# Half of a projection stage moves from plain products to seven-product pairs, and another matrix's block sums are spread over two stages

## The chip, the cores and the metric

The kernel runs on one core of one Trainium2 chip. The metric is the device time of one launch in microseconds (us); a run's time is that of one execution, and the times shown are medians of several. "The profile" is a page made from one execution recorded by the hardware profiler, and "the trace" is the record behind it. TensorE appears in it as PE (matmuls) and PEld (weight loads), VectorE as DVE, ScalarE as ACT, GpSimd as POOL, SyncE as SP (it only issues transfers here). L438 means line 438 of the kernel.

## The reference

One inference step of a two-layer hybrid decoder in float32, for 1024 prompt positions and 8 single decode positions, model width 2048. Layer A is a causal pooling mixer, layer B is sliding-window attention over keys and values projected once from layer A's output. Cut to what matters here:

```python
def pool_layer(x, ...):                       # layer A
    z = x @ w_in                              # 2048 -> 4096
    u, gate = z[..., :D_POOL], z[..., D_POOL:]
    d, new_state = multiscale_pool(u, prefix, pos)
    d = einsum(d by groups, w_grp) * scale
    y = (d * silu(gate)) @ w_out              # 2048 -> 2048
    return layer_norm(ALPHA * x + y, g_ln, b_ln), new_state

kv = h @ w_kv                                 # 2048 -> 512; rope on part of each key head

def attn_layer(x, ...):                       # layer B
    z = x @ w_in                              # 2048 -> 4096
    q = rope_partial(z[..., :D_ATTN], pos)
    gate = z[..., D_ATTN:]
    o = attn_core(q, kb, vb, q_pos, k_pos, sinks)   # window 128, 32 heads of 64, a sink per head
    y = (o * silu(gate)) @ w_out              # 2048 -> 2048
    return layer_norm(ALPHA * x + y, g_ln, b_ln)
```

## The kernel before

**Layout and precision.** Activations stand transposed, features on the 128 partitions and positions along the row, in two chunks: chunk 0 has 512 positions, chunk 1 has 520 (512 and the 8 decode positions). A feature block is 128 features; there are 16. Each float32 operand is split into a high part (a ScalarE cast, L423 for weights, L686 for inputs) and a low part (a VectorE subtraction, L438 and L695), and a product is three matmuls: high by high, high by low, low by high.

**Stages.** The list `PHASES` has nine entries: "ai" (layer A's input projection with the pooling), "ao" (its output projection), "bi" (keys, values, queries, gates and attention), "bo" (layer B's output projection), each for chunk 0 and chunk 1; "ai" of chunk 0 is in two parts. What is called the fifth stage is "bi" of chunk 0, the sixth is "bi" of chunk 1, the seventh and eighth are "bo".

**Two ways to multiply.** A unit (`unit`, L614 to L616) computes one output block of 128 features the plain way: two weight tiles of 128 x 1024, 48 matmuls with 512 columns. Two units, a pair of output blocks, can instead be had in 2 x 2 block form (halves of the features in and out, halves of the positions) by seven block products in place of eight (`seven`, L586 to L588; `pair` and `both` call it): seven weight blocks of 128 x 1024, each a quadrant of the weights or a sum of quadrants, seven input blocks, each a quadrant of the inputs or one of four sums T1 to T4, and 168 matmuls of 256 (chunk 1: 260) columns. Results are combined between the products by ScalarE and VectorE. In the kernel before, the first part of "ai" of chunk 0 and the whole fifth stage are plain (`PLAIN`); all else goes by seven products.

**Where the sums come from.** The four weight sums of a pair of blocks are formed once and kept in device memory: for w_in_a in the second part of stage one while they are used (`first_pair`; its additions are L307), for w_kv and w_in_b beside the plain units of the fifth stage (`plain_pair`, L254), for w_out_a and w_out_b by a side task (`sum_gen`, 32 pieces each, L397 to L400). When a later stage loads such a sum, `sums` runs the side task until the sum has been issued. The input sums T1 to T4 are formed by `t_ops` (four VectorE operations, L741 to L744, and a store), either on the fly or by the side task `t_gen`, which loads a stored activation.

**The order of the work.** The program is written out in one order, and `in_order` holds each engine to it. Time is counted in ticks: one tick per product of `seven`, two per weight tile of `unit` (`end`). Weights come through a stream of entries in the order of their use (`build_stream`); `begin`, called once per weight tile or product, issues loads some entries ahead, the casts and low parts fewer ahead: (7, 4, 3) in seven-product stages, (5, 4, 3) in plain ones. Inputs of the next stage are set up by `x_begin`, which first finishes the side task that makes them (`ready`); `x_tick` then loads, casts and splits them tick by tick as buffers are free, and `x_get` makes what is still missing. Side tasks (`self.side`) go one after the other, one step at every `every` ticks when at least `room` buffers are free. All of it lives in 53 buffers of 128 x 1040 floats (`Mem`).

**Attention.** Each query block t has a chain with fixed tick distances (`attend`): scores on TensorE (L1456), selection of the window and maximum (L1473, L1477, L1481), exponentials and norm on ScalarE (L1492, L1505), transposes (L1509), copies (L1518, L1519), products with the values (L1533), and the gate (L1542). Before it `q_done` fetches the rotated halves of the queries by four small transfers (`partner`, L1313, on SP's queue) and applies rope three ticks later (L1321, L1428).

**Queues.** SP issues all loads and the stores of the norms; GpSimd's queue issues the stores of weight sums, input sums and gated outputs. Each queue is in order: a load that waits for its buffer holds back what stands behind it.

Of the kernel before, what the change touches and what calls it, by code (L numbers as in the profile page):

```python
# [50 lines left out]
    ("ai", 0, (0, 1)), ("ai", 0, (1, 4)), ("ai", 1, (0, 4)), ("ao", 0, None), ("ao", 1, None), ("bi", 0, None),  # L51
    ("bi", 1, None), ("bo", 0, None), ("bo", 1, None),
# [40 lines left out]
class Slot:  # L93
# [15 lines left out]
    def free(self, stored=False):  # L109
        self.mem.release(self, 10 if stored else 0)  # L110

# [48 lines left out]
class Kern:  # L160
    def __init__(self, ctx, tc, io):
# [21 lines left out]
        self.posts, self.events, self.side = [], {}, []  # L183
        self.fresh = False
# [108 lines left out]
    def first_pair(self, name, q):  # L293
# [18 lines left out]
        def free(*ks):  # L312
# [5 lines left out]
            2: ent("e", [load("b", a21), load("c", a22)], [add("e", "b", "c", 1)], []),  # L318
# [4 lines left out]
            6: ent("c", [], [], free("c")),  # L323
# [10 lines left out]
    def build_stream(self):  # L334
        io = self.io
        w = []
        for kind, c, part in PHASES:
# [10 lines left out]
            elif kind == "bi":  # L348
                w += self.next_pairs("wkv", range(2), locked) if seven else pr("wkv", 0) + pr("wkv", 1)
                for p in range(8):  # L350
                    if seven:
                        w += pr("wib", p) + pr("wib", 8 + p)
                    else:
# [14 lines left out]
    def sum_gen(self, name):  # L368
# [15 lines left out]
        for n, (q, cs) in enumerate(parts):  # L384
            one = self.ph == "bi1"
            while one and n not in held and len(self.mem.whole()) < 6 and self.hurry is not name:
                yield
            load(n)
            if not one:
                load(n + 1)  # L390
            yield
            if one:
                yield
            s = held.pop(n)
            t = s.v(4, W)
            add = self.nc.vector.tensor_add
            add(t[:, 0:2, :], t[:, 0:2, :], t[:, 1:3, :])  # L397
            add(t[:, 2, :], t[:, 2, :], t[:, 0, :])
# [3 lines left out]
            if n % 4 == 3:  # L402
                self.summed[name] = q + 1
            yield

    def sums(self, name, q):

        self.hurry = name
        while self.summed.get(name, 16) <= q:
            self.side_step()  # L410
        self.hurry = None
# [48 lines left out]
    def end(self):  # L460
# [9 lines left out]
        room = len(self.mem.whole()) - 2 * len(self.xq)  # L470
        if self.side and int(self.i / self.every) != int((self.i - 1) / self.every) and room >= self.room:
# [156 lines left out]
    def x_begin(self, n):  # L628
# [11 lines left out]
        self.xl, self.xhi, self.xnew = [k for k in self.xq if k not in self.held], {}, {}  # L640
# [89 lines left out]
    def x_used(self, k):  # L730
        if self.last:
            for s in self.X.pop(k):
# [1271 lines left out]
```

## Time and profile before

| | |
|---|---|
| time, median of 3 runs | 2386.79 us (2384.91 to 2387.59) |
| the profiled execution's own time | 2384.47 us |
| its span, first to last instruction | 2382.7 us |
| mean granted TensorE clock | 0.996 |
| instructions in the span | 45063 |
| transfers, mean over the span | 274 GB/s |
| GpSimd busy | 192.3 us |

The stages can be told apart in the trace by the lines of their matmuls. In us from the span's start:

| stretch | from | to |
|---|---|---|
| stage one, plain part | 0 | 111.5 |
| stage one, seven-product part | 111.5 | 384.7 |
| second stage ("ai", chunk 1) | 384.7 | 755.6 |
| third and fourth ("ao") | 755.6 | 1081.8 |
| fifth ("bi", chunk 0), all plain | 1081.8 | 1561.2 |
| sixth ("bi", chunk 1) | 1561.2 | 2005.7 |
| seventh and eighth ("bo") | 2005.7 | 2382.7 |

How to read it: matmuls are pipelined and their durations overlap, so the distance from one matmul to the next is not their duration but the length of a stretch divided by the matmuls in it. An engine's idle time counts only where another engine waits for its result. A wait in the lists is written as the waiting engine and line, the engine and line waited for, the sum in us, the number of times and the longest.

### The profile page before, as it was taken

The page shows a single profiled execution, that of the slowest core. Times are in us where ns is not written, and L with a number is a line of the kernel's source. Part 1 is how long each engine was busy: PE and PEld are TensorE (multiplying, and loading weights), DVE is VectorE, ACT ScalarE, POOL GpSimd, SP SyncE. Part 2 cuts the span into 40 slices and gives each one's busy share as a digit, 9 for nine tenths or more (in the row PEclk, how much of TensorE's full clock was granted, in tenths as well). Part 3 has the DMA queues.
Part 4 walks back from the last instruction along what each step waited for, and adds up shares of the span by engine and source line. Part 5 has one row for each costly group of instructions (what it writes and reads, how often), then busy time and mean ns, then how long its engine had stood idle before and what let it go on. Part 6 is the DMA issues. An engine that isn't in the chain of part 4 may idle for free. (4 is left out here: it accounts for less than half of the span.)

```text
span 2382.7 us, 45063 instructions
## 1 busy us (share of the span) xinstructions
PE 2341.7 (98%) x17823; PEld 2198.5 (92%) x17823; DVE 1875.5 (79%) x2327; ACT 1305.6 (55%) x2363; POOL 192.3 (8%) x361
## 2 busy tenths in 40 slices
PE   8999999999999999999999999999999999999996
PEld 6899999999999999998778888899999999999996
DVE  8797999776788768868787777778777667789877
ACT  4454446454446447653564444475666667546655
POOL 0111110000000000000011111101000000000000
PEclk9999999999999999999999999999999999999998
DMA  8767779998889988988587777589786558799884
GB/s 292 243 220 277 257 255 379 310 307 299 299 297 352 313 276 313 353 294 285 186 322 261 263 269 247 202 285 303 254 244 208 173 177 296 226 337 364 303 281 141
DMA packets 250563, 653.25 MB, mean 274 GB/s; under 512 B 25456, under 2 KB 109168, under 8 KB 250352
## 3 DMA queue, kind: packets, MB, share of 16 engines
q1 hardware_dynamic: 206032, 489.50, 61.9%
q0 software_dynamic: 44320, 160.88, 17.5%
q8 instruction: 139, 2.28, 0.4%
q14 instruction: 72, 0.59, 0.1%
HBM read 459.41 MB, written 181.36 MB: 269 GB/s over the span
## 5 line engine op out<-in xcount | busy, mean ns | idle before, releaser
L586 PE MATMUL pD<-m,m 128*128 128x260 f32 (+1 forms) x4304 | 1220.8, 284 | 5.4 <-DVE m L547 3.4
L588 PE MATMUL pD<-m,m 128*128 128x260 f32 (+1 forms) x4304 | 1213.0, 282 | 2.7 <-DVE m L438 2.7
L587 PE MATMUL pD<-m,m 128*128 128x260 f32 (+1 forms) x4304 | 1213.8, 282 | 0.0
L438 DVE TENSOR_TENSOR m<-m,m 128x1024 fp32r<-128x1024 f32 x650 | 785.5, 1219 | 102.4 <-ACT m L423 69.9
L586 PEld LDWEIGHTS pD<-m,m 128*128 128x128 f32 x4304 | 810.8, 188 | 14.2 <-issue 7.6
L588 PEld LDWEIGHTS pD<-m,m 128*128 128x128 f32 x4304 | 811.3, 188 | 3.7 <-DVE m L438 3.5
L587 PEld LDWEIGHTS pD<-m,m 128*128 128x128 f32 x4304 | 810.8, 188 | 1.6 <-issue 1.4
L423 ACT CAST m<-m 128x1024 fp32r<-128x1024 f32 x650 | 676.2, 1048 | 242.8 <-DVE m L307 55.5
L614 PE MATMUL pD<-m,m 128*128 128x512 f32 x704 | 281.6, 400 | 8.0 <-ACT m L686 8.0
L615 PE MATMUL pD<-m,m 128*128 128x512 f32 x704 | 278.4, 395 | 0.8 <-DVE m L695 0.8
L616 PE MATMUL pD<-m,m 128*128 128x512 f32 x704 | 278.1, 395 | 0.0
L614 PEld LDWEIGHTS pD<-m,m 128*128 128x128 f32 x704 | 133.1, 189 | 42.7 <-ACT m L686 8.0
L615 PEld LDWEIGHTS pD<-m,m 128*128 128x128 f32 x704 | 133.2, 189 | 31.4 <-DVE m L695 1.9
L616 PEld LDWEIGHTS pD<-m,m 128*128 128x128 f32 x704 | 133.0, 189 | 30.6
L695 DVE TENSOR_TENSOR m<-m,m 128x1024 fp32r<-128x1024 f32 (+1 forms) x114 | 139.4, 1226 | 10.0 <-ACT m L686 4.3
L686 ACT CAST m<-m 128x1024 fp32r<-128x1024 f32 (+1 forms) x114 | 119.6, 1053 | 19.2 <-PE pD L616 6.2
L559 ACT COPY m<-pD 128x260 f32<-128x260 f32 (+1 forms) x75 | 28.0, 373 | 184.8 <-PE pD L588 184.4
L254 DVE TENSOR_TENSOR m<-m,m 128x1024 f32<-128x1024 f32 x88 | 107.5, 1222 | 1.9
L1492 ACT ACTIVATE m<-m,sm 128x128 f32<-128x128 f32 x256 | 99.3, 390 | 0.0
L547 DVE TENSOR_TENSOR m<-pD,m 128x260 f32<-128x260 f32 (+1 forms) x78 | 33.1, 424 | 80.7 <-PE pD L588 80.6
L954 PE MATMUL pD<-m,m 128*128 128x260 f32 (+1 forms) x528 | 91.3, 323 | 0.0
L552 DVE TENSOR_TENSOR m<-pD,m 128x260 f32<-128x260 f32 (+1 forms) x76 | 32.2, 424 | 71.1 <-PE pD L588 71.1
(197 smaller groups left out, 2136.2 us busy)
## 6 DMA issues: line engine op xcount, KB each, us to landing
m<-in_wia SPq DMA_DIRECT2D x112, 512.0 KB, 7.1
m<-in_wib SPq DMA_DIRECT2D x112, 512.0 KB, 4.9
swia<-m POOLq DMA_DIRECT2D x64, 512.0 KB, 4.8
m<-swia SPq DMA_DIRECT2D x64, 512.0 KB, 7.0
m<-swoa SPq DMA_DIRECT2D x64, 512.0 KB, 6.9
swib<-m POOLq DMA_DIRECT2D x64, 512.0 KB, 5.0
m<-swib SPq DMA_DIRECT2D x64, 512.0 KB, 5.1
m<-swob SPq DMA_DIRECT2D x64, 512.0 KB, 6.5
```

The lines of the kernel that those rows point to most:

```text
L254: self.nc.vector.tensor_add(s[out].a[:, :1024], s[a].a[:, :1024], s[b].a[:, :1024])
L423: self.nc.scalar.copy(hi.r[:, :1024], self.stream[self.cast].src().a[:, :1024])
L438: self.nc.vector.tensor_sub(lo.r[:, :1024], s.src().a[:, :1024], hi.a[:, :1024])
L586: nc.tensor.matmul(ps[:, :TH], wh[:, s], h, start=new and k == 0, stop=False, skip_group_check=on)
L587: nc.tensor.matmul(ps[:, :TH], wh[:, s], l, start=False, stop=False, skip_group_check=on)
L588: nc.tensor.matmul(ps[:, :TH], wl[:, s], h, start=False, stop=k == 7, skip_group_check=on)
L614: nc.tensor.matmul(ps[:], wh[:, s], h, start=par == 0 and k == 0, stop=False)
L615: nc.tensor.matmul(ps[:], wh[:, s], l, start=False, stop=False)
L616: nc.tensor.matmul(ps[:], wl[:, s], h, start=False, stop=par == 1 and k == 7)
L686: self.nc.scalar.copy(h.r[:, :n], s.a[:, :n])
L695: self.nc.vector.tensor_sub(l.r[:, :n], s.a[:, :n], h.a[:, :n])
L1492: nc.scalar.activation(x["s3"][:, i, :], x["s3"][:, i, :], AF.Exp, bias=nm[:, i : i + 1], scale=0.125, accum_out=rs[:, i : i + 1],)
```

## The change

The fifth stage becomes two parts, (0, 4) and (4, 8). The first keeps the plain units for keys, values and the query and gate blocks t = 0 to 7. The second computes t = 8 to 15 by seven products, with `first_pair` forming the weight sums as it goes. The stage therefore needs T1 to T4 of layer A's output for chunk 0, which a side task `t_gen` makes during the plain part, behind the norm of chunk 1.

Where a seven-product part follows a plain part of the same stage and chunk, the two input blocks that are quadrants of the odd feature blocks (numbers 4 and 5) are not loaded and split again: a `View` points into the plain part's tiles, which are freed when the last view is done. This holds for stage one as well.

```diff
+class View:
+    def __init__(self, slots, t, cs, left):
+        self.slots, self.t, self.cs, self.left = slots, t, cs, left
+    def rv(self, k, n):
+        return self
+    def __getitem__(self, at):
+        kp = at[1]
+        return self.slots[kp // 2].rv(2, self.t)[:, kp % 2, self.cs]
+    def free(self):
+        for s in self.slots:
+            self.left[s] -= 1
+            if not self.left[s]:
+                s.free()
...
+        if PHASES[n - 1] in PLAIN and PHASES[n - 1][:2] == (kind, c):
+            T = CHUNKS[c][1]
+            left = {s: 2 for j in range(4) for s in self.X[1, j]}
+            self.shared = True
+            for g in range(2):
+                tiles = list(zip(self.X[1, 2 * g], self.X[1, 2 * g + 1]))
+                for i, cs in ((5, slice(0, T // 2)), (4, slice(T // 2, T))):
+                    self.xnew[i, g] = tuple(View(t, T, cs, left) for t in tiles)
+            self.xq = [k for k in self.xq if k not in self.xnew]
```

In `first_pair` the block a22 is loaded twice: once into the buffer in which its sum is formed, and again, later, for the seventh product. So no buffer holds it in between.

```diff
-            2: ent("e", [load("b", a21), load("c", a22)], [add("e", "b", "c", 1)], []),
+            2: ent("e", [load("b", a21), load("e", a22)], [add("e", "b", "e", 1)], []),
...
-            6: ent("c", [], [], free("c")),
+            6: ent("c", [load("c", a22)], [], free("c")),
```

The sums of w_out_b are no longer one of the side tasks but a task of their own (`self.extra`), stepped at every tick. It loads one piece at a time and adds it at least three ticks later; it loads between ticks 4 and 40 of the plain part, and again from tick 8 of the sixth stage, when more than five buffers are free.

```diff
+        if name == "wob":
+            since, n = {}, 0
+            while n < len(parts):
+                hurry = self.hurry is name
+                if n in held and (hurry or self.i - since[n] >= 3):
+                    yield from add(n)
+                    n += 1
+                m = n + len(held)
+                if m < len(parts) and (not held and (self.on and len(self.mem.whole()) > 5 or hurry)):
+                    load(m)
+                    since[m] = self.i
+                yield
+            return
```

The rest is pace: in the sixth stage the look-ahead of the stream falls to (6, 3, 2) while fewer than four buffers are free; in plain parts the weight sums are formed one entry later; the norm's task has additional stops, so that its steps are smaller; side tasks take a step every 1.2 ticks in the plain part, and ten more at fixed ticks; the last attention of the plain part has its transposes 9 ticks behind its scores, the others 14.

```diff
+        if getattr(self, "ph", "") == "bi1" and len(self.mem.whole()) < 4:
+            a, b, d = min(a, 6), min(b, 3), min(d, 2)
...
-        self.make_to(self.e + b + 1)
+        self.make_to(self.e + b + (1 if self.strassen else 0))
...
-            elif (kind, c) == ("bi", 0):
+            elif (kind, c) == ("bi", 0) and not self.strassen:
+                self.summed["wob"] = 0
+                self.extra = self.sum_gen("wob")
+                for k in (4, 40):
+                    self.at(k, lambda k=k: setattr(self, "on", k == 4))
                 add(("h", 1, False), self.ln_gen(1, *acc[1], C_GA, C_BA, self.act["h", 1], self.Td.get(("h", 1))))
-                self.summed["wob"] = 0
-                add("wob", self.sum_gen("wob"))
-                self.every = 2
+                add(("h", 0, False), self.t_gen(("h", 0)))
+                for k in range(10):
+                    self.at(2 * k + 3, lambda: self.side and self.lastO < self.i - 1 and self.side_step())
+                self.every = 1.2
             elif (kind, c) == ("bi", 1):
-                self.every, self.room = 1, 99
-                self.at(14, lambda: setattr(self, "room", 0))
+                self.at(8, lambda: setattr(self, "on", True))
+                self.every, self.room = 1, 0
```

Since the sixth stage now follows a seven-product part of the other chunk, the three matmuls that `seven` puts ahead of such a start (L574) come there too.

More of the change, by code (lines that the diff above doesn't have):

```diff
@@ L382, in load, with add @@
                     self.nc.sync.dma_start(t, w[2 * q + i].rearrange("p (k n) -> p k n", k=2)[:, :, cs])
[L384 to L394, printed above, removed]
+        def add(n):
+            q, cs = parts[n]
+            s = held[n]
             t = s.v(4, W)
@@ L397, in sum_gen @@
             add(t[:, 0:2, :], t[:, 0:2, :], t[:, 1:3, :])
+            if name == "wob" and self.hurry is not name:
+                yield
+            held.pop(n)
             add(t[:, 2, :], t[:, 2, :], t[:, 0, :])
@@ L403, in sum_gen @@
                 self.summed[name] = q + 1
+        if name == "wob":
[9 more added lines that the diff above has]
+                    since[m] = self.i
+                yield
+            return
+        for n in range(len(parts)):
+            load(n)
+            load(n + 1)
+            yield
+            yield from add(n)
             yield
@@ L731, in x_used @@
         if self.last:
-            for s in self.X.pop(k):
-                s.free()
+            ss = self.X.pop(k)
+            if not (self.shared and not self.strassen and k[0] == 1):
+                for s in ss:
+                    s.free()
     def t_ops(self, E, O, dst, kp, TH):
@@ L1708, in phase_bi @@
                     self.unit(take)
-            for t in range(16):
+            for t in range(2 * ps[0], 2 * ps[-1] + 2):
                 def q_done(ps, t=t):
@@ L1854, in run @@
             elif kind == "bi":
-                self.phase_bi(c, nxt)
+                self.phase_bi(c, range(*part), nxt)
             else:
```

81 lines of the change are left out of this document (51 added, 30 removed).

## The prediction

> **What bounds the kernel now.** The page comes first: span and engine shares.
>
> ```profile
> span 2382.7 us, 45063 instructions
> PE 2341.7 (98%) x17823; PEld 2198.5 (92%) x17823; DVE 1875.5 (79%) x2327; ACT 1305.6 (55%) x2363; POOL 192.3 (8%) x361
> ```
>
> A busy share says little while matmuls overlap, so the second view is the list of waits of TensorE over the whole span: who was waited for, total us, times, longest.
>
> ```profile
> PE pD L614 <- ACT m L686: 8.0, 1, 8.0
> PE pD L586 <- DVE m L547: 3.4, 4, 1.1
> PE pD L588 <- DVE m L438: 2.7, 3, 1.2
> PE pS L1456 <- DVE m L1428: 2.6, 2, 2.3
> PE pD L586 <- ACT pD L527: 1.5, 2, 0.9
> ```
>
> All of it is under 20 us, 8.0 of them at the start. TensorE therefore sets the end with its own stream, and the time is the number of matmuls by their distance. The third view, windows, gives that distance (stretch, its length, busy us and instruction count of PE, PEld, DVE, ACT and POOL, granted clock, DMA share, GB/s):
>
> ```profile
> 1105.74:1127.97 22.23, 22.23 (x97) 18.02 (x96) 18.54 (x17) 8.92 (x10) 2.14 (x4) 1.00 0.67 210
> 111.51:190.74 79.23, 79.23 (x673) 79.23 (x672) 71.81 (x82) 39.81 (x59) 8.46 (x19) 1.00 0.68 236
> 201.97:281.19 79.22, 79.22 (x673) 79.22 (x672) 68.23 (x86) 36.91 (x56) 9.52 (x21) 1.00 0.71 251
> 292.43:373.10 80.67, 79.43 (x672) 79.23 (x671) 74.81 (x86) 43.81 (x63) 8.42 (x19) 1.00 0.78 274
> 384.72:465.20 80.48, 80.48 (x674) 80.48 (x672) 65.86 (x102) 39.83 (x65) 6.25 (x11) 1.00 0.97 354
> 1315.24:1342.34 27.10, 27.10 (x154) 21.98 (x153) 21.64 (x28) 13.05 (x34) 5.53 (x10) 1.00 0.84 292
> 1081.76:1342.34 260.58, 257.95 (x1307) 208.45 (x1306) 204.77 (x261) 130.44 (x289) 37.61 (x71) 0.99 0.76 264
> 1709.90:1734.92 25.02, 25.02 (x228) 24.25 (x226) 16.21 (x23) 16.20 (x40) 1.99 (x3) 1.00 0.83 247
> ```
>
> The first row is two plain units, which is one pair of output blocks: 96 matmuls of 512 columns in 22.23 us, 231.6 ns apart (each count has one neighbour in it). The next three are the three groups of stage one's second part, each four pairs by seven products with 256 columns: 672 matmuls in 79.2 to 80.7 us, 118 to 120 ns apart, so 19.81, 19.80 and 20.17 us for a pair. These pairs form and store their weight sums on the way, just as the new ones will. The fifth row is the same with 260 columns, 20.12 us for a pair. Row six is one step of the fifth stage: a query unit, a gate unit and one attention, 27.10; 27.10 - 22.23 leaves 4.87 for attention. The last row, a step of the sixth stage, confirms it: 25.02 - 20.12 = 4.90. The row above it is the 20 units that stay plain.
>
> **The main term.** Eight steps (t = 8 to 15) replace 768 wide matmuls by 1344 narrow ones; attention stays. At the mean of the three groups, 19.93, a pair gains 2.30 us, and eight gain **18.4**. By the fastest group it is 8 x 2.43 = 19.4, by the slowest 8 x 2.06 = 16.5.
>
> Whether the other engines keep up is worked out from the groups by line:
>
> ```profile
> L438 DVE TENSOR_TENSOR m<-m,m 128x1024 fp32r<-128x1024 f32 x650 | 785.5, 1219 | 102.4 <-ACT m L423 69.9 <-PE pD L616 7.0 <-issue 6.6
> L254 DVE TENSOR_TENSOR m<-m,m 128x1024 f32<-128x1024 f32 x88 | 107.5, 1222 | 1.9
> L1477 DVE COPY_PREDICATED m<-mki,pS 128x1024 f32<-128x1024 int32 x32 | 42.3, 1322 | 0.0
> L1519 DVE TENSOR_TENSOR m<-pS,cst 128x1024 f32<-128x1024 f32 x32 | 39.2, 1224 | 56.4 <-ACT m L1518 56.4
> L1481 DVE TENSOR_REDUCE sm<-m 128x8 f32<-128x1024 f32 x32 | 39.0, 1220 | 1.1
> L1321 DVE TENSOR_TENSOR m<-m,m 128x512 f32<-128x512 f32 x32 | 20.6, 684 | 3.8 <-DMA m<-m 3.8
> L1542 DVE SCALAR_TENSOR_TENSOR m<-pO,m 128x512 f32<-128x512 f32 x27 | 18.5, 686 | 12.6 <-PE pO L1533 12.6
> L1500 DVE RECIPROCAL sm<-sm 128x8 f32<-128x8 f32 x32 | 6.5, 203 | 1.1
> L741 DVE TENSOR_TENSOR m<-m 128x256 f32<-128x256 f32 x16 | 6.7, 417 | 0.0
> L423 ACT CAST m<-m 128x1024 fp32r<-128x1024 f32 x650 | 676.2, 1048 | 242.8 <-DVE m L307 55.5 <-DVE m L438 37.3 <-PE pO L954 24.8
> ```
>
> A new step needs on VectorE: 7 low parts and 4 weight sums, 11 x 1.22 = 13.4; attention's L1477, L1481 and L1519, 3.8; rope, output and gate, five of 0.69, 3.4; half of a tile pair's four sums (L741 on) and two combinations after products, 4 x 0.42 = 1.7; four small ones like L1500, about 0.7: **23.0 of the 24.8 us** of a step (19.93 + 4.87). Tight, but covered; the third group above had 74.81 busy in 80.67 (93%) and lost 1.4 us. The casts added on ScalarE (3 a pair, 1.05 each) lie in its 45% of idle time. Without cover, an excess on VectorE would lengthen every step by its own length.
>
> The order of the instructions also shows, for the whole program: 24 more casts and low parts of weights; 6 more of input blocks (10 for the new part; 4 fewer in stage one, which now shares tiles too); 32 sums for h0's blocks (13 us of VectorE); 20 more weight loads, 12 of them in stage one, where a22 is now read twice.
>
> **Dummy matmuls.** The sixth stage now follows a seven-product part, so three matmuls are put ahead of it. The timeline at another such place:
>
> ```profile
> 916.00 0.28 PE L588 MATMUL pD<-m,m 128*128 128x256 f32 x1
> 916.12 0.40 PE L574 MATMUL pD<-m,m 128*128 128x260 f32 x2
> 916.74 0.39 PE L574 MATMUL pD<-m,m 128*128 128x260 f32 x1 [0.22 <-ACT m L559]
> 916.97 0.28 PE L586 MATMUL pD<-m,m 128*128 128x260 f32 x1
> ```
>
> 0.97 us from the last product to the next one in place of 0.12: **+0.85**.
>
> **Hand-overs.** By the order on VectorE, seven of the new part's ten loaded input blocks get their low parts behind that of the part's first weight block; at the sixth stage's start it is 13 of 14, where it was 11. Such starts wait little today: the rows of L586 and L588 in the list of waits add up to 7.6 us, which makes at most 1.1 for each of the seven starts of seven-product parts. Two are changed: **+2.2**; lower bound 0, upper bound 8.0, the longest wait in the list.
>
> **The plain half.** Its 20 units stay, but more is put beside them: h0's sums (8 loads, 32 additions, 8 stores) must end before the new part's inputs are set up, the norm of h1 and the sums of w_out_b share the time, and SP's queue carries it all. This stretch already held the one wait inside the stage:
>
> ```profile
> 1235.09 1.29 DVE L1321 TENSOR_TENSOR m<-m,m 128x512 f32<-128x512 f32 x2 [2.05 <-DMA m<-m]
> 1236.42 0.69 DVE L1428 TENSOR_TENSOR m<-m,m 128x512 f32<-128x512 f32 x1
> 1229.92:1249.09 19.17, 16.85 (x97) 13.06 (x96) 14.95 (x23) 8.57 (x23) 2.47 (x5) 0.91 0.93 346
> 1261.05:1276.19 15.14, 15.14 (x97) 12.13 (x96) 14.87 (x19) 5.66 (x14) 2.89 (x5) 1.00 0.90 342
> 755.60:797.94 42.34, 42.34 (x361) 42.34 (x360) 35.48 (x46) 21.22 (x28) 3.98 (x6) 1.00 1.00 371
> m<-m SPq DMA_DIRECT2D x64, 64.0 KB, 4.2
> m<-in_wib SPq DMA_DIRECT2D x112, 512.0 KB, 4.9
> ```
>
> Rope waited 2.05 us for its swapped tile, whose four small transfers stand in SP's queue behind large loads; the scores (L1456, first list) wait for rope, and the products behind the scores on TensorE wait too. The unit took 19.17 instead of 15.14, **4.03 us** for a 2.3 us wait, since the granted clock was 0.91 for the rest of it.
>
> [...]
>
> How often will it happen? I counted the transfers: over the stage's first 32 weight blocks (keys, values and six steps, about 208 us) the changed program issues 69.8 MB and the kernel before 53.4, so 336 GB/s are asked for in place of 257. At 342 one step passed free, at 346 one lost 4.03, and at 371 plain products ran on unhurt. Bounds: -4.0 (even today's wait goes) and +20.2 (all six steps wait, five more than now). I take one more, **+4.0**, nearer the lower end, because no queue saturates and h0's sums come in small steps.
>
> **Edits costed at nothing.** Second a22 loads: stage one's DMA share is 0.68 to 0.78 in the rows above; exposed, each would cost about a landing (4.9). w_out_b's sums now run to the end of the sixth stage; VectorE is at 16.21 of 25.02 there. If they came late, the first loads of the seventh stage would wait a load plus a store, some 10 us (two of 4.9). The shorter look-ahead in the sixth stage at under four free buffers keeps one low part (1.22 us) ahead of a product of 2.87 (20.12 / 7).
>
> **Sum.** -18.4 + 0.85 + 2.2 + 4.0 = -11.3. Against the profiled execution's own 2384.47 that is 2373.2; the median of the runs, 2386.79, lies 2.3 above it, so **2375.4** is forecast. With each term at its bounds the mechanism spans about 2364 to 2384 (the upper end leaves three more waits).
>
> **Rivals.**
> *Rope waits at most steps* (0.10): four more waits, 16.1 in place of 4.0, give 2387.5, no change. For: the asked rate rises by 30%, and rope's lag of three ticks is unchanged. Against: the step at 342 GB/s.
> *Transfers pace the plain half* (0.10), the other side. The place is the same 32 blocks; 69.8 MB must pass in 208 us. Rate by share is 371 in the row above but 247 / 0.83 = 298 in row 1709.90, whose transfers are small. At 298 they take 234, +26: -18.4 + 3.05 + 26 = +10.7, **2397.5**. It decides below 69.8 / (208 + 15.4) = 312 GB/s. Against it: 342 and more seen in this very stage.
> *VectorE paces the new half* (0.02): 23.0 us grow by waits to the old 27.10 and the change does not do what it says; no gain, 2390 with the small terms.
> *All clear* (0.17): no added wait and today's gone: -19.4 + 0.85 - 4.0 = -22.6, 2364.2.
> *Weight loads come to the surface* (0.01). A load lasts 188 ns and there are 576 more:
>
> ```profile
> L587 PEld LDWEIGHTS pD<-m,m 128*128 128x128 f32 x4304 | 810.8, 188 | 1.6 <-issue 1.4
> ```
>
> End to end, 1344 x 0.188 = 252.7 against 177.8 now: +75, about 2469 with the other terms. The narrow rows above, 118 ns for a load with its matmul, speak against it. [...]
>
> **Chances.** The forecast gets 0.60; with the rivals' chances that makes 1. A measurement of this kernel tells about 0.2% from no change, 4.8 us, so faster means under 2382.0 and slower over 2391.6. Faster: the forecast less its slow end beyond 2382 (0.02), and all clear, 0.75. Same: that slow end, rope's waits, VectorE's pace, 0.14. Slower: transfers and loads, 0.11. The range, 2364 to 2390, takes in all but the slower cases and what lies under all clear; the forecast's own is 2364 to 2384.
>
> **What would show it.** Right: steps of about 24.8 us in the second half of the fifth stage, narrow matmuls 118 to 120 ns apart, plain pairs still 22.2; one or two waits of the scores on rope in the plain half, each with a granted clock under 1. Wrong: steps near 27 with VectorE full (third rival); a plain half longer than today's 260.6 us by 20 or more, with a DMA share near 1 (transfers); waits for input blocks at the two hand-overs adding up to over 8 us.

## The result, and the profile after

The changed kernel takes 2391.05 us (median of 17 runs, 2385.79 to 2393.85); the kernel before, run beside it, 2385.76 (17 runs, 2381.74 to 2391.45). The ratio is 1.0018, 95% interval 1.0011 to 1.0024: no gain, and by the interval a small loss, some 3 to 6 us. The forecast was 11 us of gain, and the time lies 1 us above the range. By the bound of 0.2% it is still no change, at the upper edge.

The page of the changed kernel, span and engine shares. (Lines have moved: seven products are L631 to L633, plain ones L659 to L661, low parts L479 and L751, casts L464 and L742, `first_pair`'s sums L328, scores L1517, values L1594.)

```profile
span 2388.0 us, 46500 instructions
PE 2328.6 (98%) x18402; PEld 2217.1 (93%) x18402; DVE 1921.7 (80%) x2389; ACT 1335.7 (56%) x2411; POOL 197.1 (8%) x369
```

TensorE's busy time fell by 13.1 us, from 2341.7, but the span grew by 5.3. The difference is in its waits: all of them together are 40.3 us, 21.9 before. The largest (sum, times, longest):

```profile
PE pD L659 <- ACT m L742: 8.1, 1, 8.1
PE pS L1517 <- DVE m L1489: 7.2, 5, 2.9
PE pD L631 <- ACT pD L572: 6.1, 5, 2.2
PE pD L633 <- DVE m L479: 5.7, 5, 2.4
PE pD L631 <- DVE m L592: 3.8, 4, 1.4
```

The first is the start, as before. Scores on rope rose from 2.6 to 7.2, a product that waits for the combination before its own (L572) from 1.5 to 6.1, the low part of a weight (L479) from 2.7 to 5.7. The windows tell in which stage (plain part, new part, sixth stage, stage one's seven-product part; then three steps of the new part; columns as before):

```profile
1085.50:1350.21 264.71, 259.70 (x1307) 209.60 (x1305) 224.78 (x306) 128.68 (x282) 43.73 (x81) 0.99 0.87 306
1350.21:1555.03 204.82, 199.21 (x1789) 191.63 (x1787) 177.02 (x204) 136.84 (x311) 25.61 (x51) 1.00 0.73 249
1555.03:2009.80 454.77, 447.25 (x3999) 433.18 (x3997) 335.78 (x443) 298.40 (x689) 26.81 (x42) 1.00 0.78 246
111.63:387.17 275.54, 272.49 (x2165) 265.73 (x2164) 237.68 (x285) 134.72 (x194) 32.90 (x71) 1.00 0.82 286
1430.07:1454.93 24.86, 24.77 (x226) 23.93 (x225) 20.39 (x24) 15.74 (x39) 3.00 (x6) 1.00 0.68 215
1479.72:1504.63 24.91, 24.84 (x226) 24.00 (x225) 20.39 (x24) 15.83 (x39) 2.99 (x6) 1.00 0.57 173
1504.63:1529.35 24.72, 24.72 (x226) 23.94 (x225) 22.50 (x28) 16.77 (x40) 3.55 (x7) 1.00 0.78 280
```

The same stretches in the kernel before, beside the 260.58 of its plain half shown above:

```profile
1342.34:1561.25 218.91, 218.91 (x1250) 177.36 (x1248) 161.24 (x211) 108.67 (x277) 32.76 (x61) 1.00 0.71 241
1561.25:2005.71 444.46, 443.52 (x3958) 430.54 (x3957) 322.46 (x413) 290.68 (x664) 21.30 (x34) 1.00 0.73 235
111.50:384.71 273.21, 271.97 (x2164) 265.43 (x2163) 244.24 (x292) 137.16 (x196) 32.80 (x71) 1.00 0.75 264
```

The steps of the new part run as worked out, 24.7 to 24.9 us. The new part as a whole is 14.1 shorter than the eight plain steps, but the sixth stage is 10.3 longer. Part of that is work passed on: one attention's transposes and products with the values now fall behind the boundary (41 more matmul records in the sixth stage). So the two stretches are best read together:

| stretch | forecast | measured |
|---|---|---|
| stage one, seven-product part | 0 | +2.3 |
| plain half of the fifth stage | +4.0 | +4.1 |
| new part and sixth stage | -15.35 | -3.8 |
| all other stages | 0 | +2.7 |
| sum | -11.3 | +5.4 |

The first three lines are differences of the rows; the fourth is what is left, before rounding, of the 5.4 by which the profiled execution (2389.83 us) exceeds that of before. TensorE's waits in the sixth stage alone, after,

```profile
PE pD L631 <- ACT pD L572: 3.2, 3, 1.4
PE pD L633 <- DVE m L479: 2.4, 1, 2.4
PE pS L1517 <- DVE m L1489: 2.0, 2, 1.2
```

make 7.6 us; the same list of before has one line:

```profile
PE pD L586 <- ACT pD L527: 0.9, 1, 0.9
```

VectorE's timeline beside the longest of them (start, duration, line, idle time before it and what ended that) shows its cause:

```profile
1854.09 0.23 DVE L1737 SCALAR_TENSOR_TENSOR m<-pO,sgd 128x64 f32<-128x64 f32 x1 [0.55 <-PE pO L1728]
1858.46 2.54 DVE L479 TENSOR_TENSOR m<-m,m 128x1024 fp32r<-128x1024 f32 x2 [4.14 <-DMA o<-m]
```

L1737 is the last operation of a decode step. Its result is stored (L1741, the transfer `o<-m`), and its buffer is given back at once, without the mark that a store still reads it. The planner hands it to the next weight's low part, and VectorE stands 4.14 us until the store has landed. At the hand-over into the new part VectorE and with it ScalarE stood for a different reason:

```profile
1341.34 1.23 DVE L328 TENSOR_TENSOR m<-m,m 128x1024 f32<-128x1024 f32 x1 [3.18 <-DMA m<-in_wib]
1354.18 1.23 DVE L1580 TENSOR_TENSOR m<-pS,cst 128x1024 f32<-128x1024 f32 x1 [3.25 <-ACT m L1579]
```

The first weight sum of the new part waits for its load from w_in_b; all that stands behind it, input blocks' low parts and an attention's probabilities, comes late, and TensorE waits four times, 4.9 us in all:

```profile
PE pD L632 <- DVE m L751: 1.7, 1, 1.7
PE pD L631 <- DVE m L592: 1.4, 1, 1.4
PE pO L1594 <- ACT m L1579: 1.0, 1, 1.0
PE pO L1594 <- DVE m L1580: 0.8, 1, 0.8
```

### The profile page after: what moved, and what is told of

It reads as the page before. It is cut to its first block, busy times and chain, and to the rows that moved or that the text cites. A ratio compares the mean times of both kernels' runs of the same rounds, so it can differ in the third digit from the quotient of the medians.

```text
span 2388.0 us, 46500 instructions
## 1 busy us (share of the span) xinstructions
PE 2328.6 (98%) x18402; PEld 2217.1 (93%) x18402; DVE 1921.7 (80%) x2389; ACT 1335.7 (56%) x2411; POOL 197.1 (8%) x369
## 5 line engine op out<-in xcount | busy, mean ns | idle before, releaser
L631 PE MATMUL pD<-m,m 128*128 128x260 f32 (+1 forms) x4752 | 1348.2, 284 | 11.6 <-ACT pD L572 6.1
L633 PE MATMUL pD<-m,m 128*128 128x260 f32 (+1 forms) x4752 | 1339.5, 282 | 5.7 <-DVE m L479 5.7
L632 PE MATMUL pD<-m,m 128*128 128x260 f32 (+1 forms) x4752 | 1339.1, 282 | 1.7 <-DVE m L751 1.7
L631 PEld LDWEIGHTS pD<-m,m 128*128 128x128 f32 x4752 | 894.7, 188 | 24.1 <-issue 13.0
L633 PEld LDWEIGHTS pD<-m,m 128*128 128x128 f32 x4752 | 895.1, 188 | 7.2 <-DVE m L479 6.9
L632 PEld LDWEIGHTS pD<-m,m 128*128 128x128 f32 x4752 | 894.9, 188 | 3.6 <-DVE m L751 1.9
L479 DVE TENSOR_TENSOR m<-m,m 128x1024 fp32r<-128x1024 f32 x674 | 814.3, 1219 | 99.2 <-ACT m L464 57.4
L464 ACT CAST m<-m 128x1024 fp32r<-128x1024 f32 x674 | 701.3, 1048 | 321.0 <-DVE m L328 65.3
L659 PE MATMUL pD<-m,m 128*128 128x512 f32 x448 | 179.1, 400 | 8.1 <-ACT m L742 8.1
L660 PE MATMUL pD<-m,m 128*128 128x512 f32 x448 | 176.9, 395 | 1.2 <-DVE m L751 1.2
L661 PE MATMUL pD<-m,m 128*128 128x512 f32 x448 | 176.8, 395 | 0.0
L751 DVE TENSOR_TENSOR m<-m,m 128x1024 fp32r<-128x1024 f32 (+1 forms) x120 | 146.9, 1226 | 5.9 <-ACT m L742 5.4
L742 ACT CAST m<-m 128x1024 fp32r<-128x1024 f32 (+1 forms) x120 | 125.7, 1052 | 11.6 <-PE pD L660 5.2
L659 PEld LDWEIGHTS pD<-m,m 128*128 128x128 f32 x448 | 84.5, 189 | 29.8 <-ACT m L742 8.4
L592 DVE TENSOR_TENSOR m<-pD,m 128x260 f32<-128x260 f32 (+1 forms) x86 | 36.5, 424 | 86.7 <-PE pD L633 86.6
L328 DVE TENSOR_TENSOR m<-m,m 128x1024 f32<-128x1024 f32 x80 | 97.8, 1222 | 8.9 <-DMA m<-in_wia 4.4
L660 PEld LDWEIGHTS pD<-m,m 128*128 128x128 f32 x448 | 84.6, 189 | 21.3 <-DVE m L751 2.2
L661 PEld LDWEIGHTS pD<-m,m 128*128 128x128 f32 x448 | 84.4, 188 | 19.6
L1015 PE MATMUL pD<-m,m 128*128 128x260 f32 (+1 forms) x528 | 91.5, 323 | 0.0
L1015 PEld LDWEIGHTS pD<-m,m 128*128 128x128 f32 x528 | 79.5, 188 | 8.2
```

The lines of the kernel that those rows point to most:

```text
L464: self.nc.scalar.copy(hi.r[:, :1024], self.stream[self.cast].src().a[:, :1024])
L479: self.nc.vector.tensor_sub(lo.r[:, :1024], s.src().a[:, :1024], hi.a[:, :1024])
L631: nc.tensor.matmul(ps[:, :TH], wh[:, s], h, start=new and k == 0, stop=False, skip_group_check=on)
L632: nc.tensor.matmul(ps[:, :TH], wh[:, s], l, start=False, stop=False, skip_group_check=on)
L633: nc.tensor.matmul(ps[:, :TH], wl[:, s], h, start=False, stop=k == 7, skip_group_check=on)
L659: nc.tensor.matmul(ps[:], wh[:, s], h, start=par == 0 and k == 0, stop=False)
```

## The experiments

Each is compared with the kernel before, run on the same chip. The ratio of the changed kernel to hold against is 1.0018; the changed kernel itself was not run again beside the experiments. A profile is of one execution, which can lie several us from the median of its runs.

### The second load of a22 (three runs)

The smallest part of the change by itself, put into the kernel before; it bears on stage one alone:

```diff
-            2: ent("e", [load("b", a21), load("c", a22)], [add("e", "b", "c", 1)], []),
+            2: ent("e", [load("b", a21), load("e", a22)], [add("e", "b", "e", 1)], []),
...
-            6: ent("c", [], [], free("c")),
+            6: ent("c", [load("c", a22)], [], free("c")),
```

> The kernel before with a22 loaded twice in stage one, one part of the change alone. If the added loads cost: 2 to 3 us over the kernel before. If they are hidden behind a DMA share of 0.68 to 0.78: within 1 us.

The kernel took 2390.96 us (12 runs), ratio 1.0022 (1.0013 to 1.0031): some 5 us, more than either side had given it. The row of stage one's seven-product part:

```profile
111.73:386.56 274.83, 272.10 (x2164) 265.38 (x2163) 243.86 (x292) 136.45 (x195) 32.88 (x71) 1.00 0.82 287
```

The DMA share rises from 0.75 to 0.82, as in the changed kernel, and 1.6 of the 5 us are in this stretch. Where the rest arises, the one profile does not settle: it is the slowest of its runs (2396.23), and 8.0 us of its excess stand in the sixth stage, which the edit does not touch.

The reverse, in the changed kernel: a22 loaded once everywhere.

> The changed kernel with a22 loaded once again in every pair that forms its sums (stage one and the new part). If the 20 added loads cost (first and second stage were 3.2 us longer in the profile), it is 2 to 4 us faster than the changed kernel, 2387 to 2389; if those 3.2 us are scatter between executions, it is within 1.5 us of 2391, or slower because a buffer less is free in the new part.

It took 2389.89 us (12 runs), 1.0017 (1.0005 to 1.0028): no gain over the changed kernel. Stage one's part was back at 273.6, and the new part, where the block now holds its buffer, was not longer (203.5). But the profiled run shows a wait of 7.7 us for a low part in the seventh stage, behind 7.9 us in which VectorE stood for a load of the attention's output. Whether that comes with this order or was chance is not shown. The third variant keeps the second load in the new part alone:

```diff
+        if name == "wia":
+            return {
...
+                2: ent("e", [load("b", a21), load("c", a22)], [add("e", "b", "c", 1)], []),
...
+                6: ent("c", [], [], free("c")),
+            }
```

> The changed kernel with a22 loaded once in stage one as before, and twice only in the new part. If the second loads in stage one cost what the earlier run of that part alone showed (5 us by its median, one wait of 2 us at the end of stage one in its profile): the wait of about 2.2 us near 361 us goes, the seven-product part of stage one is 273 to 274 us in place of 275.5, the time 2386 to 2389. If not: within 1.5 us of 2391.

It took 2386.08 us (10 runs), 0.9999 (0.9987 to 1.0010): 4.5 us less than the changed kernel (0.0019 of 2386). With e4 this makes the loads in stage one a cost of 4 to 5 us, found from both sides.

The other profiles show where most of it goes. In the changed kernel and its variants this stretch takes 273.6 to 273.7 us with the block loaded once (e3, e6, e8, e10, e11). Loaded twice it takes 275.5 and 276.0 (the changed kernel, e9), or, where the clock was halved behind the wait at its end (last section), 277.0 to 277.3 (e1, e2, e5, e7), as here in e7:

```profile
111.58:388.81 277.23, 273.99 (x2164) 267.28 (x2163) 237.92 (x285) 134.89 (x194) 32.80 (x71) 0.99 0.82 286
```

That wait, 2.2 us for a combination on ScalarE (L572), is not one for a late transfer. ScalarE stood earlier, at a cast:

```profile
355.51 1.04 ACT L464 CAST m<-m 128x1024 fp32r<-128x1024 f32 x1 [7.15 <-DVE m L597]
```

The loads of w_in_a before it had landed by 350.6 in the trace. By the instruction list the cast writes into the buffer that the combination L597 on VectorE is the last to read, and L597 stands behind four steps of the pooling. With the block loaded once the same cast follows its own sum on VectorE, 4.0 us earlier (351.48 in e10). So most of the cost comes through the buffers that the added load shifts.

### The sums of w_out_b (two runs)

If the side task's pieces beside the sixth stage are what makes it longer, moving them all ahead, into the third and fourth stages, should free it:

```diff
                 self.every = 2
+                self.summed["wob"] = 0
+                self.extra = self.sum_gen("wob")
+                self.on = True
             elif (kind, c) == ("ao", 1):
...
-                self.summed["wob"] = 0
-                self.extra = self.sum_gen("wob")
-                for k in (4, 40):
-                    self.at(k, lambda k=k: setattr(self, "on", k == 4))
...
-                self.at(8, lambda: setattr(self, "on", True))
```

Without the shorter look-ahead of the sixth stage, and then with it:

> The changed kernel with the 32 pieces of w_out_b's sums moved ahead, into the third and fourth stages, and without the shorter look-ahead in the sixth. Buffer theory (the sixth stage's 10 us come from pieces that hold buffers there and from the shorter look-ahead): the sixth stage falls from 454.8 us to about 447, its waits of TensorE from 7.5 us to about 1; the third and fourth stages, where 12 to 14 buffers are free, grow by 0 to 4; in all 2384 to 2388, 3 to 7 us under the changed kernel. Rival (the sixth stage is longer because its inputs are set up later at the hand-over from the new part): it stays over 452 us.

> As e1, but the shorter look-ahead of the sixth stage is kept. Buffer theory: with the pieces gone, four buffers are nearly always free, so the look-ahead is hardly ever shortened, and it equals e1 within 1.5 us. If the shorter look-ahead by itself costs, it is 2 us or more over e1.

They took 2410.3 and 2408.88 us (4 runs each), ratios 1.0101 (1.0087 to 1.0115) and 1.0094 (1.0080 to 1.0108). The total was missed by over 20 us. The windows of the first (third, fourth, sixth stage):

```profile
760.30:941.27 180.97, 167.97 (x1353) 165.06 (x1352) 145.16 (x179) 87.28 (x116) 18.75 (x28) 0.97 0.97 351
941.27:1115.53 174.26, 167.53 (x1353) 164.43 (x1353) 146.60 (x165) 96.11 (x129) 15.17 (x25) 0.99 1.01 382
1582.34:2030.95 448.61, 446.45 (x3999) 433.11 (x3997) 305.86 (x374) 296.75 (x689) 10.07 (x19) 1.00 0.62 197
```

and of the kernel before, third and fourth stage:

```profile
755.60:916.96 161.36, 161.14 (x1353) 159.83 (x1352) 126.50 (x139) 87.04 (x115) 9.39 (x15) 1.00 0.88 306
916.96:1081.75 164.79, 164.79 (x1353) 162.70 (x1353) 131.41 (x126) 97.07 (x129) 4.93 (x11) 1.00 0.92 330
```

The sixth stage did what was expected: 448.6 instead of 454.8, its waits down to 2.5 us. But the third and fourth, whose transfers already took 0.88 and 0.92, ran full and grew by 19.6 and 9.5. VectorE's waits there name stores of the sums that had not landed (13.3 us) and loads of w_out_b (5.3), so full transfers and the buffers held by them act together; the two were not separated. The two variants agree within 1.5 us, with intervals that overlap. So the shorter look-ahead costs nothing that can be seen without the pieces; what it costs beside them, where fewer buffers are free, was not tested. Half of the theory stood (the pieces are what the sixth stage waits behind), and the place chosen for them was worse.

### The decode step's buffer

The pieces stay in the sixth stage; only the buffer's mark is added:

```diff
             x["v"].free(True)
-            W.free()
+            W.free(True)
```

> The changed kernel with one edit: the decode step's buffer is marked as still being stored when it is freed. If the waits near 1858 in the sixth stage come from a low part put into that buffer while its store runs: they go (2.4 and 1.4 us), the sixth stage falls from 454.8 to 449.5 to 451, and the time by 3 to 5 us, to 2386 to 2388. If they come from the shorter look-ahead or from the pieces of w_out_b as such, they stay on other buffers and the time is within 1.5 us of 2391.

It took 2384.18 us (11 runs), 0.9999 (0.9990 to 1.0009): by the ratio 4.5 us less than the changed kernel, within the 3 to 5 expected. Its sixth stage and its waits there:

```profile
1551.43:2002.09 450.66, 446.86 (x3999) 433.18 (x3998) 335.64 (x443) 298.42 (x689) 26.75 (x42) 1.00 0.78 249
```

```profile
PE pS L1517 <- DVE m L1489: 2.1, 2, 1.3
PE pD L631 <- ACT pD L572: 1.7, 2, 0.9
```

The wait for L479 is gone, and of the stage's excess 4.1 us. The other profiles agree: 453.7 to 456.3 where the pieces stand in the stage and the mark is missing (the changed kernel, e3, e5, e6, e7), 449.4 to 450.7 with it (e8 to e11). The buffer was given back this way in the kernel before too, and no wait followed; with the pieces beside the decode steps fewer buffers are free, and this one is taken at once.

### The loads of the plain half

VectorE stood before the first weight sum because in plain parts a load is issued five entries ahead and the sum formed four ahead, one entry between them. Six ahead, in the fifth stage's plain part alone:

```diff
-        a, b, d = self.ahead if self.strassen else (5, 4, 3)
+        a, b, d = self.ahead if self.strassen else (6 if self.ph == 'bi0' else 5, 4, 3)
```

> The changed kernel with weight loads of the plain half issued six entries ahead in place of five. If the hand-over's waits (5.4 us in the new part's first 30 us) come from VectorE standing 3.2 us before a weight sum whose load has not landed: that wait and the two behind it shrink, the new part falls from 204.8 to 200 to 203 us. If the hand-over is bound by VectorE's own work or by buffers: the new part stays at 204 to 206, or the plain half grows by waits for buffers.

It took 2383.7 us (10 runs), 0.9991 (0.9982 to 1.0001): 6.4 us less than the changed kernel. The new part took 201.6 instead of 204.8 (where the other 3 us came from, its profile, 4.5 above the median, does not show), and the list of waits at the hand-over is down to two:

```profile
PE pD L631 <- DVE m L592: 1.4, 1, 1.4
PE pD L632 <- DVE m L751: 0.8, 1, 0.8
```

### Scores later (three runs)

The waits of the scores on rope: what if the scores come two ticks later in the plain part?

```diff
-                self.attend(c, t, 8, 14 if t <= 2 * ps[-1] else 9, 2)
+                self.attend(c, t, 10, 14 if t <= 2 * ps[-1] else 9, 2)
```

In this kernel the transposes of the plain part's last query block are overwritten by the next scores; the work in it is the same.

> The changed kernel with the plain half's attention chains started two ticks later, so that rope has two ticks more between its small transfers and the scores that wait for it. Rope theory (the plain half's 4 us are two waits of the scores on rope, each followed by 3.4 us at half the clock): both waits go, the plain half falls from 264.7 to about 257, below the 260.6 of the kernel before, and the time from 2391 to 2384 or so. Rival (it is general lateness of VectorE and transfers, which then shows elsewhere): the plain half stays over 262, with waits on other lines.

It took 2392.07 us (10 runs), 1.0028 (1.0015 to 1.0041): no gain. The one profile is the fastest of its runs (2383.57), so it cannot show what the median lost. In it the plain half was 260.01, between the 257 of the one theory and the 262 of the other. The waits of scores on rope fell from 7.2 to 1.8 over the span, and the next link took part of them over, values that wait for the copied probabilities, 0.8 in the changed kernel, here:

```profile
PE pO L1594 <- DVE m L1580: 3.7, 3, 1.7
```

This shift together with the a22 variant and the buffer's mark (the last block's transposes are overwritten here too):

> e5 and e6 together, and the decode step's buffer marked as still being stored when it is freed, so that the next low part is not put into it while its store runs. Separate losses add up: plain half about 257, stage one's seven-product part about 273.5, and in the sixth stage the wait of 2.4 us on VectorE near 1860 with the 1.4 after it gone, 450 to 452 in place of 454.8; in all 2378 to 2382, faster than the kernel before by 4 to 8. Rival: the waits move elsewhere, and it stays over 2386.

It took 2388.68 us (10 runs), 1.0004 (0.9992 to 1.0016). Two edits that gave 4.5 us each gave 3.3 together with the shift, against the 9 to 13 expected. Next, the a22 variant, the buffer's mark and the loads six ahead, with the scores one tick later and the last chain's transposes one tick nearer:

> As e10, with the plain half's scores one tick later (the last chain keeps its place). If rope's lateness still costs there, the plain half is 1 to 4 us shorter than in e10. If the lateness moves on to the values, as it did with two ticks, it equals e10 within 1.5 us.

It took 2384.41 us (11 runs), 1.0001 (0.9991 to 1.0011), 7.9 us worse than the same kernel without the shift (next section; 0.0033 of 2385). Its plain part and the wait that does it:

```profile
1083.99:1353.23 269.24, 261.05 (x1306) 210.68 (x1305) 225.61 (x307) 130.09 (x286) 44.66 (x83) 0.98 0.85 304
```

```profile
PE pO L1604 <- DVE m L1590: 7.6, 2, 5.4
```

Scores on rope waited 1.8 in the whole of this run; the lateness did not vanish, it came out at the values (L1604), longer than before.

### The three mends together, and what is the change's own

The a22 variant, the loads six ahead and the buffer's mark, with the scores where they were:

> Three edits on the changed kernel: a22 twice in the new part only, weight loads of the plain half six entries ahead, the decode step's buffer marked as being stored. If each loss has its own cause they add up: seven-product part of stage one 273.7, plain half 260 to 263, new part about 201.6, sixth stage about 450, in all 2376 to 2380, 6 to 10 us under the kernel before. If the waits move elsewhere, as rope's did, it stays at 2383 or more.

It took 2378.35 us (9 runs, 2374.88 to 2380.68), 0.9968 (0.9956 to 0.9980), as expected and faster than both kernels. Stage one, plain half, new part and sixth stage:

```profile
111.64:385.34 273.70, 272.58 (x2165) 266.06 (x2163) 237.38 (x285) 134.95 (x193) 32.79 (x71) 1.00 0.75 264
1084.47:1343.71 259.24, 256.50 (x1306) 207.41 (x1305) 225.30 (x306) 130.88 (x288) 44.66 (x83) 1.00 0.87 315
1343.71:1545.38 201.67, 198.76 (x1789) 191.60 (x1788) 176.29 (x203) 134.46 (x307) 24.45 (x49) 1.00 0.74 248
1545.38:1994.75 449.37, 447.09 (x3999) 433.50 (x3997) 335.56 (x443) 298.43 (x689) 26.75 (x42) 1.00 0.77 250
```

Against the kernel before: +0.5, -1.3, and -12.3 for the last two (651.04 to 663.37). The profiled execution as a whole is 8.8 us shorter, so the other stages took 4.4 more, most of it in the second (372.8 for 370.9) and the seventh (180.5 for 179.0); that was not traced. Singly the mends gave 4.5, 6.4 and 4.5 against the changed kernel, 15.4 in all; together 11.9 (0.0050 of 2386). Two of them can also be made in the kernel before, whose fifth stage is plain throughout:

> The kernel before, with two of the three mends of the mended version and nothing of the change: weight loads six entries ahead in place of five in the whole (plain) fifth stage, and the decode step's buffer marked as stored. If the mends repair what the change itself broke (hand-over into the new part, the buffer that the side task's pieces run into), the kernel before has little for them to repair: its fifth stage stays at 479.5 and its sixth at 444.5, time 2383 to 2387, and the mended version's gain of 7.4 is the change's own, uncovered. If the mends are general improvements that have nothing to do with the change, the kernel before gains as much as the changed one did by the two of them (several us): 2376 to 2380, and the split is worth nothing.

It took 2383.7 us (12 runs), 0.9987 (0.9978 to 0.9995), between the two theories. Fifth and sixth stage:

```profile
1082.15:1558.17 476.02, 475.53 (x2554) 384.92 (x2552) 365.97 (x472) 239.62 (x566) 70.39 (x132) 1.00 0.73 256
1558.17:2004.16 445.99, 444.12 (x3958) 430.80 (x3957) 322.79 (x413) 290.59 (x664) 21.30 (x34) 1.00 0.71 234
```

The fifth stage, 479.49 in the kernel before, lost the one wait of the scores on rope and what followed it; the sixth gained nothing. So some 3 us of the mended version's 7.6 can be had without the change, by this one profile through the earlier loads, and about 4.5 (0.9968 / 0.9987 = 0.9981) remain for the change itself. The two intervals just touch.

## Why the prediction was wrong, step by step

**The main term was right.** Steps of 24.72 to 24.91 were forecast as 24.8; less 4.87 for the attention, their narrow matmuls lie 118 to 119 ns apart. VectorE was busy 20.4 to 22.5 of a step against the 23.0 worked out. Neither VectorE's pace nor the weight loads became the bound: the loads of the 1344 more narrow products lasted 188 ns each (L631 to L633), as before, and the distance of the products did not grow by them.

**Dummy matmuls** cost what was put down: 1553.94 to 1555.03, 1.09 us from the last product of the new part to the first of the sixth stage in place of 0.12, +0.97 for +0.85.

**The plain half came out at its number by luck.** It was +4.1 for the forecast's +4.0: two waits of the scores on rope (2.1 and 2.9 us), each with the granted clock at 0.50 for 3.41 us (last section), where one of 2.3 was. But only the second has the forecast's mechanism, four small transfers that land late:

```profile
1297.24 1.29 DVE L1382 TENSOR_TENSOR m<-m,m 128x512 f32<-128x512 f32 x2 [5.98 <-DMA m<-m]
1184.11 1.29 DVE L1382 TENSOR_TENSOR m<-m,m 128x512 f32<-128x512 f32 x2
```

The second row is the rope ahead of the first wait. VectorE had no idle time before it: the small transfers had landed by 1182.6, and it worked until 1184.1 at the norm of chunk 1, a low part and input sums, the work put beside the plain units. And the size does not recur. In profiles whose edits lie in other stages the half took 261.23 (e9) and 259.56 (e6), with waits of the scores of 4.5 and 3.3 us in all and the clock never halved there (its mean 1.00 in the half of e6, 0.997 over the whole of e9). The row of e6:

```profile
1083.62:1343.18 259.56, 256.23 (x1306) 207.42 (x1305) 224.59 (x306) 128.50 (x282) 43.58 (x81) 1.00 0.87 312
```

So against the 260.58 of before the half costs between -1.0 and +4.1, by how long these waits last and whether the clock falls. The rate was 306 to 312 GB/s with a share of 0.87; transfers did not pace the half, as their rival had it. Of the remedies, a later reader passes the wait on (e8, e11). Whether earlier loads help here is not shown: the scores waited 3.3 us in e7 and 2.2 in the mended version, but 3.3 in e6 as well, without them.

**Hand-overs were mis-sized.** 2.2 us for two starts, by waits of today's starts; measured 4.9 for one of them, at the new part. Most of today's starts stand behind a seven-product part, where a load is issued two entries ahead of its sum (seven and five); here a plain part stands ahead, with one entry between. One start in the kernel before was like it, stage one's, and VectorE stood there too, for a load of w_in_a:

```profile
100.78 1.23 DVE L307 TENSOR_TENSOR m<-m,m 128x1024 f32<-128x1024 f32 x1 [5.32 <-DMA m<-in_wia]
```

TensorE did not wait behind it, so the list of TensorE's waits, by which the term was priced, could not show it. In the new part an attention and most of the input blocks stand behind such a wait. That the low parts would queue behind the first weight block's was in the text, that this block itself would wait for its load was not. With the loads one entry earlier the waits are 2.2 (e7).

**The step that failed is "Edits costed at nothing".** It named three covers, and two did not hold.
First, the second a22 loads in stage one, hidden "at a DMA share of 0.68 to 0.78": they cost 4 to 5 us (e4, e6). The prediction looked for their price in the transfers; most of it lay in a buffer. At the end of this part a product waited 2.2 us for a combination, a wait that is in the profile of every kernel here with the loads doubled there (1.9 to 2.2) and of none without, and behind it is a cast into a buffer that VectorE had not yet read.
Second, w_out_b's sums in the sixth stage, checked for VectorE's time alone (16.21 of 25.02; the step after it had 21.93): VectorE had the time, 335.8 of 454.8 us in this stage, the buffers were short. Waits grew by 6.7 us. Moving the pieces away takes the stage to 448.6 (e1), marking one buffer takes it to 450.7 with the pieces in place (e9). So the pieces are the condition, and the early return of a buffer with a store under way is the mechanism of the larger part (3.8 of the 6.7 us of waits). The late event that the prediction feared instead, sums missing at the start of the seventh stage, did not come.
Third, the shorter look-ahead: nothing without the pieces (e1 and e2); beside them it stays open.

The balance: of the 11.6 us by which new part and sixth stage miss their -15.35, the hand-over has 2.7 (4.9 for 2.2) and the sixth stage's waits 6.7; some 2 us, as well as the 2.7 spread over the other stages, were not traced. No rival described this outcome: each took one price of the fifth stage to its end, none the side work's costs in the stages around it. Two readings of the prediction were also off, without weight for the outcome: the row at 371 GB/s is of seven-product pairs, not of plain products, and the clock of 0.91 is the mean over its stretch, in which it was 0.50 for 3.41 us (1238.52 to 1241.93) and full otherwise.

## What to carry to other kernels

When work is moved off the bound engine's path, ask what it holds, not only which engine it keeps busy: in a fully planned kernel the scarce thing was buffers, and one that was given back a store too early cost as much as a quarter of the main term (4.5 of 18.4 us). A mean transfer share of 0.75 says nothing of the buffers that an added load shifts; price it by a run of that edit alone. Where a wait comes from late data, moving its source earlier helped (e7, where the waits at the hand-over fell from 4.9 to 2.2 us), while moving the reader later passed the wait to the next link (e5, 0.8 to 3.7 us), and in e11 made it longer (one of 5.4 us). And a profile that meets a forecast to a tenth can be luck: look at other executions of the same stretch.

## What was not expected of the hardware

A short wait of TensorE cost twice here. At the two waits of the scores the granted clock was halved for 3.41 us and then full again (rows as before; the windows do not fit the halved time exactly, so they show 0.52 and 0.53; cut to 1186.23 to 1189.64 and to 1298.87 to 1302.28, they show 0.50):

```profile
1186.00:1189.41 3.41, 3.24 (x16) 2.57 (x16) 3.38 (x6) 2.19 (x4) 0.00 (x0) 0.53 1.03 408
1299.00:1302.41 3.41, 3.10 (x16) 2.52 (x16) 3.38 (x8) 0.00 (x0) 0.55 (x1) 0.52 0.00 0
1302.41:1305.00 2.59, 2.59 (x14) 1.93 (x11) 2.59 (x4) 2.19 (x3) 0.53 (x1) 1.00 0.65 164
358.00:368.00 10.00, 7.78 (x67) 7.58 (x66) 9.97 (x9) 9.38 (x15) 0.53 (x1) 1.00 0.97 318
1858.00:1868.00 10.00, 6.85 (x55) 6.64 (x56) 7.93 (x11) 6.97 (x24) 0.71 (x1) 1.00 0.63 178
```

The waits were 2.1 and 2.9 us. In the kernel before, the wait of 2.32 us and half of the 3.41 us at 0.50 make the 4.03 us that its unit took longer. The last two rows hold waits of 2.2 and 2.4, after which the clock stayed full (1.00). The wait of 2.2 at 361 recurs in the same place in six profiles: in four of them (e1, e2, e5, e7) the clock was halved behind it, in two (the changed kernel and e9) not. So by these profiles it is partly chance, and it costs: stage one's part took 277.0 to 277.3 us in those four (in e7 at a mean clock of 0.99) and 275.5 and 276.0 in the two (1.00 in the changed kernel). It may be one source of the scatter of several us between runs of one kernel; how much of that it makes was not shown. The length of the wait alone does not tell the outcome: 2.1 us were enough in one place, 2.4 were not in another.

Transfers added to stretches that were already near full were dear. In e1 the third and fourth stages, at shares of 0.88 and 0.92 before, moved 63.5 and 66.6 MB instead of 49.4 and 54.4 (rate by length of the rows), 26.3 MB more, and took 29.1 us more: 1.1 us for each added MB, with the buffers that they held in it.
